# A two-layer hybrid decoder trunk: another way of finding the instruction order of four engines

## The chip, the cores and the metric

The kernel runs on one core of one Trainium2 chip, in one launch. The metric is the device time of that launch in microseconds (us). TensorE (PE) does the matrix products and transposes, VectorE (DVE), ScalarE (ACT) and GpSimd (POOL) the rest; transfers are issued by SyncE (SP), and a few by ScalarE. Every engine takes its instructions in the order of its own list, and waits at the head of the list until what the instruction needs is done.

## The reference

Two layers over one sequence of 1024 tokens of width 1024, all in f32. A layer normalises its input, projects it to 3088 columns, which three groups of heads share, and projects their outputs back:

```python
mod = c_act @ w_mod + b_mod                       # c_act = silu(c), one row
shift, scale, gate = jnp.split(mod[:, None, :], 3, axis=-1)
h = rms_norm(x, pre_gain) * (1.0 + scale) + shift
proj = h @ w_in                                   # split into aq..ag, rq..rg, gq..gg, ga
a_out = sliding_window_attention(rotary(aq), rotary(ak), av, sinks) * silu(ag)   # 8 heads, window 128
r_out = rms_norm(retention(rotary(rq), rotary(rk), rv)) * silu(rg)               # 4 heads, chunks of 128
log_a = log_sigmoid(ga @ gla_gate_w + gla_gate_b) / 16
g_out = rms_norm(gated_linear_attention(gq, gk, gv, log_a), gla_norm_gain) * silu(gg)   # 4 heads
y = concat([a_out, r_out, g_out]) @ w_out
x = x + gate * rms_norm(y, post_gain)
```

The modulation `mod` depends on `c` alone, but its weights w_mod are 1024 x 3072 for each layer.

## The kernel before

**Tiles.** The tokens lie in 8 tiles of 128. Every product of f32 values is done as products of a rounded high part and a low part in fp32r (`hi`, `lo`), three passes of TensorE in all. The high and low parts of weights and of the normalised, transposed input lie in two large arenas (`arena`); a weight is brought by a transfer into a stage buffer (`st`, 128 x 512 f32, 256 KB), and converted: `hi` by a copy (L149 on ScalarE, L151 or L529 on VectorE), `lo` by a subtraction (L533, on VectorE or GpSimd). All through the kernel there are five stage buffers (BST = 5) in rotation.

**Stages of a layer.** `pre` makes the normalised input of a tile: squares (L651), the sums (L640, L634), a power on GpSimd (L635), the scaling (L666), transposes on TensorE (L180), the modulation (L698, L700) and its split into high and low (L704, L708). Then come the projections of twelve column groups. Around them: SiLU gates (L984, L986), the decays of the gated-linear heads (`gla_decays`, L1038 to L1059), the rotation of queries and keys (`rotary`, L817 to L822; decay factor L1148) with tables that the kernel computes itself (L432 to L449), retention (L1170 to L1191), the gated-linear core (`gla_core`: 32-column products on TensorE, masked copies L1112, state L1133, L1134), attention by runs of tiles (L833 to L934), and the output projection, norm and residual (L1198 to L1239). Finished heads go through DRAM (`mixS`, `mixF`).

**Modulation.** The gate of layer 0 and the whole modulation of layer 1 are computed beside the projections, as sums on VectorE: each 256 KB piece of w_mod comes through a stage buffer, and one instruction (L362, L364) multiplies it by a column of `c_act` and adds it to `acc`:

```python
for k in range(KT):
    wt = stage()
    dma("lwm", wt, w_mod[l, j, hh, :, k, :])
    if k == 0 and j < 2:
        V.tensor_scalar(acc, wt, c_act[:, k:k + 1], None, ALU.mult)
    else:
        V.scalar_tensor_tensor(acc, wt, c_act[:, k:k + 1], acc, ALU.mult, ALU.add)
    yield lat("mod2", l)
```

**What sets the order.** The program is written as one stream of TensorE work and a set of jobs (generators). A clock that counts TensorE's cost decides when a job goes on (`pump`, with the delays of the table `L`; `mod2` is 4.0), and so where its instructions stand in the program. For TensorE, program order is the order on the chip (`manual_schedule` for PE). For the other engines and for the transfers the tile framework's scheduler chooses the order when the program is built: it takes instructions whose inputs it holds to be ready by a model of time, and inserts the waits. Buffers of a pool are handed out again when their last reader is done, so a transfer into a stage buffer waits for the instruction that read it last. The transfers lie on eight lanes, and on each lane one waits until the one ahead of it has landed.

## Time and profile before

| | |
|---|---|
| median of 3 runs | 1000.36 us (999.89 to 1002.28) |
| profiled execution | 1005.29 us, its span 1003.6 us |
| granted TensorE clock, mean | 0.989 |
| TensorE busy | 972.6 us, 97% of the span |
| VectorE busy | 683.7 us, 68% |
| ScalarE busy | 409.0 us, 41% |
| GpSimd busy | 234.7 us, 23% |
| VectorE waiting for pieces of w_mod at L364 | 12.0 us in 11 waits, longest 3.2 us |

The profile shows one execution. Its page gives the busy time of each engine, the chain of work that ended last, the groups of instructions by line and tile, and the transfers. A line number is that of the listing; helpers such as `copy` (L149, L151), `dma` (L154), `mult` (L165) and `transp` (L180) stand for many callers, which the tile's name tells apart. The timeline gives instructions in order of time with the idle time ahead of each and what ended it; the windows give busy time of the engines by stretch.

### The profile page before, as it was taken

How to read it: one execution, taken by the hardware profiler on the slowest of the kernel's cores; microseconds unless marked ns; L12 is line 12 of the kernel's file. 1: busy time of each engine (PE TensorE's matmuls, PEld its weight loads, DVE VectorE, ACT ScalarE, POOL GpSimd, SP SyncE). 2: the span in 40 equal slices, each digit the busy share in tenths (PEclk: the TensorE clock that was granted, in tenths of full speed). 3: DMA queues.
4: the chain of work that ended last, by engine and by line, in shares of the span. 5: the costliest groups of instructions: out<-in, count | busy, mean ns of one | idle time of the engine just before them, and what ended most of it. 6: DMA issues, size and time to landing. Idle time of an engine off the chain costs nothing.

```text
span 1003.6 us, 19610 instructions
## 1 busy us (share of the span) xinstructions
PE 972.6 (97%) x7137; PEld 827.5 (82%) x7137; DVE 683.7 (68%) x1680; ACT 409.0 (41%) x1152; POOL 234.7 (23%) x275
## 2 busy tenths in 40 slices
PE   5899999999999999999999999999999999999896
PEld 1599999888998777778889999998999777777675
DVE  3788857678666778654677385775766577566786
ACT  2486312233332656632555332133333267563231
POOL 2310001223320234420122010122332034444000
PEclk8899999999999999999999999999999999999998
DMA  8842513623235355597555241352222435477883
GB/s 306 297 145 79 166 43 102 189 78 121 65 94 172 90 156 168 167 283 234 178 171 166 82 139 32 117 171 68 64 82 88 122 91 153 129 227 237 252 272 132
DMA packets 112172, 148.73 MB, mean 148 GB/s; under 512 B 11998, under 2 KB 63688, under 8 KB 112076
## 3 DMA queue, kind: packets, MB, share of 16 engines
q1 hardware_dynamic: 106380, 137.92, 44.2%
q10 hardware_dynamic: 5696, 9.56, 2.6%
q8 instruction: 56, 0.92, 0.4%
q14 instruction: 40, 0.33, 0.1%
HBM read 109.17 MB, written 36.18 MB: 145 GB/s over the span
## 4 chain that ended last, share of the span: by engine, by line
PE 80%; DMA 8%; DVE 7%; issue 2%; POOL 1%; ACT 1%; SPq 1%; ACTq 0%; POOLq 0%; DVEq 0%
PE mm L165 62%; PE aux L165 14%; PE aux L180 5%; DMA st<-in_w_in_dram 2%; DMA st<-in_w_last_dram 1%; POOL sm L635 1%; DMA xk<-in_x_dram 1%; DMA a<-mixS 1%; DMA t<-aoS 1%; DMA t<-mixF 1%; DVE arena L533 1%; DVE t L328 0%; SPq L154 0%; DMA t<-in_x_dram 0%; DMA t<-xs 0%
## 5 line engine op out<-in xcount | busy, mean ns | idle before, releaser
L165 PE MATMUL mm<-arena 128*128 128x256 f32 (+2 forms) x1824 | 300.0, 318 | 1.8 <-ACT arena L704 1.8
L165 PE MATMUL mm<-arena,arena 128*128 128x256 f32 (+2 forms) x1824 | 299.0, 317 | 0.0
L165 PEld LDWEIGHTS mm<-arena 128*128 128x128 f32 x1824 | 255.3, 191 | 26.6 <-issue 4.1
L165 PEld LDWEIGHTS mm<-arena,arena 128*128 128x128 f32 x1824 | 252.9, 188 | 25.2 <-issue 4.4
L635 POOL TENSOR_TENSOR sm<-sm,mhalf 128x1 f32<-128x1 f32 (+1 forms) x64 | 55.8, 871 | 347.0 <-DVE sm L634 328.4
L165 PE MATMUL mm<-arena,mx 128*128 128x512 f32 (+1 forms) x564 | 132.6, 392 | 3.7 <-ACT kept L1332 3.7
L165 PEld LDWEIGHTS mm<-arena,mx 128*128 128x128 f32 x564 | 103.0, 190 | 28.2 <-ACT kept L1332 4.2
L149 ACT ACTIVATE t<-aux 128x256 f32<-128x256 f32 (+2 forms) x124 | 55.7, 467 | 74.9 <-PE aux L180 63.8
L149 ACT ACTIVATE arena<-st 128x512 fp32r<-128x512 f32 x94 | 55.9, 626 | 54.8 <-DMA st<-in_w_in_dram 19.7
L533 POOL TENSOR_TENSOR arena<-st,arena 128x512 fp32r<-128x512 f32 x31 | 43.3, 1399 | 134.1 <-ACT arena L149 96.8
L923 POOL TENSOR_TENSOR smx<-smx,sm 128x512 f32<-128x512 f32 x32 | 36.5, 1142 | 127.6 <-DVE sm L922 118.4
L533 DVE TENSOR_TENSOR arena<-st,arena 128x512 fp32r<-128x512 f32 x77 | 59.5, 794 | 4.5 <-ACT arena L149 2.4
L919 ACT ACTIVATE smx<-smx,sm 128x129 f32<-128x129 f32 x128 | 49.9, 392 | 28.8 <-DVE sm L916 28.8
L180 PE MATMUL aux<-c_ident,t 128*128 128x128 f32 (+1 forms) x292 | 48.8, 284 | 5.8 <-DVE t L666 5.5
L364 DVE SCALAR_TENSOR_TENSOR acc<-st,c_act,acc 128x512 f32<-128x512 f32 x60 | 45.5, 759 | 12.6 <-DMA st<-in_w_mod_dram 12.0
L180 PEld LDWEIGHTS aux<-c_ident,t 128*128 128x128 f32 (+1 forms) x292 | 35.4, 145 | 13.5 <-DVE t L666 7.4
L698 ACT ACTIVATE t<-aux,mod,mod 128x128 f32<-128x128 f32 x68 | 26.0, 460 | 44.5 <-DVE t L1239 18.3
L165 PEld LDWEIGHTS aux<-t,mx 32*128 32x128 f32 (+1 forms) x896 | 39.5, 187 | 3.9 <-issue 1.9
L967 ACT ACTIVATE t<-aux 128x256 f32<-128x256 f32 x32 | 12.3, 384 | 73.3 <-PE aux L165 60.7
L165 PE MATMUL aux<-t,mx 32*128 32x32 f32 (+1 forms) x896 | 40.6, 272 | 0.0
L914 DVE COPY_PREDICATED smx<-c_curmask,aux 128x256 f32<-128x256 int32 x64 | 25.5, 447 | 18.9 <-ACT smx L149 15.8
L1239 DVE SCALAR_TENSOR_TENSOR t<-t,sm,t 128x512 f32<-128x512 f32 x32 | 23.9, 779 | 17.9 <-DMA t<-in_x_dram 12.3
(220 smaller groups left out, 1378.2 us busy)
## 6 DMA issues: line engine op xcount, KB each, us to landing
st<-in_w_in_dram SPq DMA_DIRECT2D x96, 256.0 KB, 3.7
st<-in_w_mod_dram SPq DMA_DIRECT2D x64, 256.0 KB, 3.0
mx<-mixS SPq DMA_DIRECT2D x20, 512.0 KB, 5.8
mixS<-t SPq DMA_DIRECT2D x72, 128.0 KB, 2.6
st<-in_w_last_dram SPq DMA_DIRECT2D x36, 256.0 KB, 3.7
wm<-in_w_mod_dram SPq DMA_DIRECT2D x12, 512.0 KB, 7.2
t<-in_x_dram SPq DMA_DIRECT2D x24, 256.0 KB, 4.3
t<-tabS SPq DMA_DIRECT2D x16, 256.0 KB, 3.7
```

What stands on the lines that cost most here:

```text
L149: A.activation(dst, src, AF.Copy)
L165: T.matmul(dst, lhsT, rhs, start=start, stop=stop)
L180: T.transpose(dst, src, idn)
L364: V.scalar_tensor_tensor(acc, wt, c_act[:, k:k + 1], acc, ALU.mult, ALU.add)
L533: e.tensor_tensor(lo, st, f(hi), ALU.subtract)
L635: G.tensor_tensor(r, r, mhalf[:, :w], ALU.pow)
L698: A.activation(hf[:, ks], at[kt], AF.Identity, scale=gain, bias=shift)
L914: V.copy_predicated(sv, curmask.unsqueeze(1).to_broadcast((P, 2, P)), pv[:, :, n // P - 1, :])
L919: A.activation(sm[:, h, :], sm[:, h, :], AF.Exp, bias=mx[:, h:h + 1], accum_out=sums[:, h:h + 1])
L923: eng("pn").tensor_tensor(sm[:, :, 0:128], sm[:, :, 0:128], rs.unsqueeze(2).to_broadcast((P, 4, P)), ALU.mult)
L967: A.activation(sq, po, AF.Square)
L1239: V.scalar_tensor_tensor(xt[j], yg[j], r, xt[j], ALU.mult, ALU.add)
```

## The change

The context in which the whole program is built gets one option. With it, the scheduler that orders ScalarE, VectorE, GpSimd and the transfers finds out what is ready by playing the program through its timeline model, in place of the simple model of before. TensorE stays under `manual_schedule`. Tiles, buffers, arithmetic and the choice of the engine for each instruction are not touched.

```diff
-    with tile.TileContext(nc) as tc:
+    with tile.TileContext(nc, schedule_with_timeline_sim=True) as tc:
         with tc.manual_schedule(engines={mybir.EngineType.PE}):
             trunk(tc, ins, cst, out)
```

## The prediction

> **What bounds the kernel now.** I read the page first: the busy shares and the chain that ended last, then its groups of instructions and its transfer table.

> ```profile
> PE 972.6 (97%) x7137; PEld 827.5 (82%) x7137; DVE 683.7 (68%) x1680; ACT 409.0 (41%) x1152; POOL 234.7 (23%) x275
> PE 80%; DMA 8%; DVE 7%; issue 2%; POOL 1%; ACT 1%; SPq 1%; ACTq 0%; POOLq 0%; DVEq 0%
> L364 DVE SCALAR_TENSOR_TENSOR acc<-st,c_act,acc 128x512 f32<-128x512 f32 x60 | 45.5, 759 | 12.6 <-DMA st<-in_w_mod_dram 12.0
> st<-in_w_in_dram SPq DMA_DIRECT2D x96, 256.0 KB, 3.7
> st<-in_w_mod_dram SPq DMA_DIRECT2D x64, 256.0 KB, 3.0
> ```

> TensorE (PE) is busy 972.6 of the 1003.6 us, so all its waits together are 31 us: that is the most any order of the other engines could give back. TensorE's own order is written by hand and is the same in both builds. What the change can do, then, is to shorten these 31 us or to add to them. The third row names the danger. The modulation sums (L364) are on VectorE (DVE), each needs a 256 KB piece of w_mod that lands 3.0 us after its issue, and VectorE stands 12.0 us in front of them already. While it stands there everything behind it in its order stands too. Each piece is in one of five stage buffers, which the projection weights (w_in) use as well, and the next piece into a buffer is issued only when the last reader of that buffer is done. Where two pieces of w_mod follow each other through one buffer, their sums can't be closer than one round trip.

> Next I read the windows (stretch; length, busy us of PE, PEld, DVE, ACT, POOL; granted clock; DMA share; GB/s), to see where TensorE waits and what VectorE has in hand there.

> ```profile
> 0.00:25.00 25.00, 13.78 (x33) 4.77 (x34) 8.89 (x24) 6.23 (x13) 5.62 (x14) 0.88 0.87 306
> 25.00:50.00 25.00, 21.36 (x103) 13.78 (x102) 19.14 (x40) 11.63 (x31) 8.66 (x9) 0.85 0.84 296
> 75.00:100.00 25.00, 25.00 (x200) 24.01 (x200) 22.41 (x47) 16.59 (x38) 1.79 (x2) 1.00 0.25 77
> 300.00:525.00 225.00, 225.00 (x1227) 175.40 (x1226) 151.60 (x310) 110.04 (x330) 56.83 (x66) 1.00 0.58 181
> 950.00:1004.00 54.00, 45.27 (x205) 36.64 (x204) 39.31 (x74) 13.69 (x34) 4.37 (x6) 0.95 0.63 205
> ```

> Of the 31 us, 11.2 + 3.6 are in the first 50 us and 8.7 in the last 54. Between 300 and 525 us there is none, with VectorE two thirds busy: there, lateness of a few us costs nothing unless it passes the slack. From 75 to 100 us VectorE is busy 22.4 of 25 us, so what it loses before, it can't make up.

> **The change, part by part.** The instructions are the same, but for one table load of ScalarE (ACT) more. Put side by side, the two builds' lists differ on VectorE in 1599 of some 1620 lines, on SyncE (SP) in 503, on ScalarE in 471, on GpSimd (POOL) in 146, on TensorE in none. The one pattern I find is that instructions which consume a transfer, L364 and the weight conversions (L149, L151, L529, L533), come earlier, ahead of work that TensorE waits for. For each such place I take the durations of before, add what is newly ahead of the instruction TensorE needs, add the wait for a landing, and take off the slack it had.

> *Start-up.* The normalised tiles 2 and 3 (L666) feed TensorE's transposes.

> ```profile
> 44.86 0.88 DVE L666 TENSOR_SCALAR t<-mx,sm 128x512 f32<-128x512 f32 x2 [0.44 <-POOL sm L635]
> 46.99 1.88 DVE L666 TENSOR_SCALAR t<-mx,sm 128x512 f32<-128x512 f32 x2 [0.45 <-POOL sm L635]
> 48.53 1.09 PE L180 MATMUL aux<-c_ident,t 128*128 128x128 f32 x8 [0.65 <-DVE t L666]
> 37.69 10.60 SPq L715 DMA_DIRECT2D t<-in_x_dram  x8
> 49.76 0.76 SPq L772 DMA_DIRECT2D gnc<-in_gla_norm_gain_dram  x1
> ```

> TensorE already waits 0.65 us for the second pair, so there is no slack. Newly ahead of the first pair are 2.75 us of VectorE (two L529, an L151 and two L533 among them), of the second 2.19 us. Among these are L774, which needs gnc, and L151 of a weight piece. On SyncE gnc, three constants and that piece move past x loads, which in before were queued for 10.6 us. So 2.2 us is the work alone; if the loads come late too, 5. I take 3.0, nearer the work.

> *Tables and the first rotations.* L449 copies a table tile that TensorE transposes at 110.08.

> ```profile
> 106.35 0.27 DVE L820 TENSOR_TENSOR tr<-mm,sincos 128x128 f32<-128x128 f32 x1
> 107.95 0.41 DVE L449 COPY t<-sincos 128x512 f32<-128x512 f32 x1
> 110.08 0.60 PE L180 MATMUL aux<-c_ident,t 128*128 128x128 f32 x4
> 104.41 6.70 SPq L154 DMA_DIRECT2D st<-in_w_mod_dram  x4
> ```

> Three L364, one L533 and three rotary steps (3.32 us) are newly ahead of L449. The second L364 stands ahead of L820 too; its piece, issued at 104.41, lands at 107.4, 1.05 us after L820's old start. Slack was 110.08 − 108.36 = 1.72. That makes 3.32 + 1.05 − 1.72 = 2.65 us; if start-up backlog is still there, which the busy 75 to 100 us suggest, up to 8. I take 4.0.

> *The gated-linear heads at 220 us, the clearest place.* Masked copies (L1112) feed 32-column products at 223.17.

> ```profile
> 220.05 0.75 DVE L364 SCALAR_TENSOR_TENSOR acc<-st,c_act,acc 128x512 f32<-128x512 f32 x1 [0.27 <-DMA st<-in_w_mod_dram]
> 221.50 0.90 DVE L1112 COPY_PREDICATED mx<-c_mask,aux 128x128 f32<-128x128 int32 x4 [0.70 <-ACT mx L1111]
> 223.62 0.75 DVE L364 SCALAR_TENSOR_TENSOR acc<-st,c_act,acc 128x512 f32<-128x512 f32 x1 [1.23 <-DMA st<-in_w_mod_dram]
> 220.82 0.33 SPq L154 DMA_DIRECT2D st<-in_w_mod_dram  x1
> 224.40 4.83 SPq L154 DMA_DIRECT2D st<-in_w_mod_dram  x2
> 223.17 1.54 PE L165 MATMUL aux<-t,mx 32*128 32x32 f32 x48
> ```

> The rows show one buffer going round: sum at 220.05, next issue 220.82, next sum 223.62, next issue 224.40. That is 3.57 us a round. The other four buffers hold weights whose place in the arena TensorE hasn't left. In the new order three more L364 stand back to back ahead of the first L1112: at 223.6, 227.2 and 230.8. L1112 starts at 231.5 instead of 221.5, 10.0 us late. Its first copy had 1.4 us of slack, so TensorE stands still for 8.6 us. Nothing covers it, since TensorE's order is fixed. One more L364 stands ahead of the next group (L1077, L1078, L1087): of its 3.57 us I count 1.5.

> *What a standstill does to the clock.* The trace has a like one, at 940 us (the first row is the wait, the others are windows).

> ```profile
> 939.99 4.61 PE L165 MATMUL mm<-arena,mx 128*128 128x512 f32 x12 [3.72 <-ACT kept L1332]
> 940.00:941.00 1.00, 1.00 (x3) 0.86 (x4) 1.00 (x3) 0.00 (x0) 0.00 (x0) 0.71 0.54 149
> 941.00:942.00 1.00, 1.00 (x4) 0.71 (x4) 1.00 (x2) 0.39 (x1) 0.00 (x0) 0.50 0.79 192
> 942.00:943.00 1.00, 1.00 (x4) 0.81 (x3) 0.75 (x3) 0.33 (x2) 0.00 (x0) 0.50 0.72 195
> 943.00:944.00 1.00, 1.00 (x5) 0.77 (x4) 0.29 (x4) 0.00 (x0) 0.57 (x1) 0.58 0.88 276
> ```

> After 3.72 us without work the granted clock is 0.71, 0.50, 0.50 and 0.58: 0.29 + 0.50 + 0.50 + 0.42 = 1.7 us of work lost. I add 1.7 us once, for the standstill at 223. [...]

> *From layer 0 to layer 1.* On ScalarE three conversions L149, each waiting for its weight piece, are newly ahead of the squares (L651) of the next tiles; on VectorE an L364 and four L700 (2.03 us) are newly ahead of an L986.

> ```profile
> 529.01 0.62 ACT L651 ACTIVATE t<-t 128x512 f32<-128x512 f32 x1
> 525.39 9.37 SPq L154 DMA_DIRECT2D st<-in_w_in_dram  x7
> 538.56 0.41 DVE L986 SCALAR_TENSOR_TENSOR t<-t,mm 128x256 f32<-128x256 f32 x1
> 540.86 0.75 DVE L364 SCALAR_TENSOR_TENSOR acc<-st,c_act,acc 128x512 f32<-128x512 f32 x1 [0.61 <-DMA st<-in_w_mod_dram]
> 535.08 1.09 PE L180 MATMUL aux<-c_ident,t 128*128 128x128 f32 x8
> 540.26 1.05 PE L165 MATMUL mm<-arena 128*128 128x272 f32 x7
> ```

> L364 can't run before its landing at 540.86; with it (0.75) and the L700 (1.36) ahead, L986 starts at 543.0 and ends at 543.4, and TensorE wanted it at 540.26: 3.1 us. The third L149 waits for about 525.4 + 2 + 3.7 = 531, where L651 ran at 529.0; through L640, L634, GpSimd's power and L666 these 2 us reach the transposes at 535.08, which have no slack. Between 0 and 2.6 I count 1.4: together 4.5.

> *Rotations of layer 1.*

> ```profile
> 589.98 0.42 DVE L1148 TENSOR_TENSOR t<-t,c_kdec 128x256 f32<-128x256 f32 x1
> 593.28 0.60 PE L180 MATMUL aux<-c_ident,t 128*128 128x128 f32 x4
> 662.76 0.41 DVE L1148 TENSOR_TENSOR t<-t,c_kdec 128x256 f32<-128x256 f32 x1
> 665.75 0.60 PE L180 MATMUL aux<-c_ident,t 128*128 128x128 f32 x4
> ```

> Newly ahead of the first L1148 are four L364 and a rotary step, 3.15 us, with 2.9 us of slack: 0.3 us if all pieces have landed, 7.3 if each is issued as late as before. I take 2.0, since two of them free their buffers earlier too. Ahead of the second are 4.47 us (four L533, an L151, an L364 and two others) with 2.6 us of slack: 1.9.

> *At nothing* I cost the attention stretch, the mix stores and loads that SyncE reorders, GpSimd's changes and the added table load: the work that hides them is TensorE's unbroken 225 us and its like. If that cover is gone at one place it costs 1 to 3 us; the end part, where TensorE waits already, is the likeliest.

> The sum is 3.0 + 4.0 + 8.6 + 1.5 + 1.7 + 4.5 + 2.0 + 1.9 = 27.2 us on an execution of 1005.29, 2.7%. The runs shown have a median of 1000.36, so the profiled one is 0.5% above it; in the same proportion 1000.36 becomes 1027.

> **The rivals.**

> *Little of it counts (chance 0.18).* A standstill of TensorE lets VectorE catch up, and pieces issued earlier land earlier. Then the start (2.2 us) is left and, of 220 us, between a quarter of the 8.6 us and all of it with the 1.7 of clock: 4.4 to 12.5 us, 1005 to 1013. For it: the attention stretch swallows anything. Against it: the round of 3.57 us.

> *Everything counts (0.07).* Every upper end together: 5 + 8 + 8.6 + 3.6 + 1.7 + 5.7 + 7.3 + 1.9 is 42 us, and two or three waits more that pass the 3.7 us of the row at 940 add 1.7 each: 1042 to 1047. Against it: a late buffer is also one that TensorE has left.

> *Faster (0.13).* Transfers consumed earlier free their buffers earlier, so the next weights are there before TensorE asks. Its place is where TensorE waits in before: 0.65 us at 48.5, 3.72 + 1.7 at 940 and 8.7 in the last 54 us, 14.8 in all. If a fifth to a half of that goes and the round at 220 us doesn't form, because a second buffer is free there, it is 3 to 7 us faster, 993 to 997. It decides when L364 at 223.6 finds its piece landed. Against it: in before, with an order that freed buffers later, that instruction waited 1.23 us; and the first waits of the start-up hang on loads that don't move.

> *No difference (0.06).* TensorE at 97% hides all of it, or the moved instructions run in the same relative order where it matters: 997.4 to 1003.4. That the change does nothing is out, by the lists.

> **How the numbers follow.** The forecast, waits for landings ahead of work that TensorE needs, gets 0.56: 1027 by the sum; from 1014 (the low ends, half of the 8.6 us and no loss of clock: 2.2 + 2.65 + 4.3 + 3.1 + 0.3 + 1.9 = 14.4 us) to 1042 (the upper ends). 1000 to 1045 leaves out the faster case (0.13), part of no difference and most of the worst, together 0.2. A measurement of this kernel can tell about 0.3%, 3 us, from no change; faster by more 0.13, within 0.06, slower 0.81.

> **What would show it.** Right: TensorE's idle before L165 aux<-t,mx near 223 + shift at 7 us or more, ended by L1112, with VectorE waiting on three pieces of w_mod one after another and the clock at half after it; VectorE's wait for w_mod well above 12.0 us; TensorE's idle time near 58 us in all. Each place shows by its own row: L666 near 50, L449 near 115, L986 near 555, L1148 near 610 and 690. Wrong: TensorE's idle at or under 31 us, or L1112 released by ScalarE as before.

## The result, and the profile after

The changed kernel takes 1031.16 us (median of 4 runs, 1028.88 to 1034.67), the kernel before, in the runs set beside it, 1000.57 us: a ratio of 1.0303 (95% interval 1.0277 to 1.033). The forecast was 1027. The profiled execution of the changed kernel is its fastest, 1028.88 us with a span of 1027.1. The profiled execution of before that the prediction used (1005.29) is slower than its other runs, so I took a second profile of the same order (the kernel same_order, below; span 997.1). Times of single places are compared with that one.

The page of the changed kernel, in the same rows as before:

```profile
PE 979.5 (95%) x7137; PEld 832.8 (81%) x7137; DVE 692.3 (67%) x1680; ACT 408.6 (40%) x1153; POOL 236.1 (23%) x275
PE 72%; DVE 12%; DMA 9%; issue 3%; ACT 2%; POOL 1%; SPq 1%; DVEq 0%; POOLq 0%; ACTq 0%
L364 DVE SCALAR_TENSOR_TENSOR acc<-st,c_act,acc 128x512 f32<-128x512 f32 x60 | 47.4, 789 | 23.6 <-DMA st<-in_w_mod_dram 23.1
```

TensorE is idle 1027.1 − 979.5 = 47.6 us where it was 31 (25.7 in same_order). In the chain VectorE has gone from 7 to 12%, TensorE from 80 to 72. VectorE's wait for pieces of w_mod has gone from 12.0 us (13.6 in same_order) to 23.1 us. Both builds have the same instructions, but for the one table load more on ScalarE; what differs is their order.

TensorE's waits in its timeline name the places (start, duration, instruction, idle time ahead of it and what ended it):

```profile
49.41 2.22 PE L180 MATMUL aux<-c_ident,t 128*128 128x128 f32 x16 [1.50 <-DVE t L666]
101.31 0.66 PE L180 MATMUL aux<-c_ident,t 128*128 128x128 f32 x4 [0.98 <-DVE t L449]
115.60 0.66 PE L180 MATMUL aux<-c_ident,t 128*128 128x128 f32 x4 [1.41 <-DVE t L449]
236.03 2.95 PE L165 MATMUL aux<-t,mx 32*128 32x32 f32 x44 [8.01 <-DVE mx L1112]
265.66 0.67 PE L165 MATMUL aux<-stG,t 128*128 128x256 f32 x2 [1.47 <-DVE mx L1112]
323.33 0.30 PE L180 MATMUL aux<-c_ident,t 128*128 128x128 f32 x1 [1.20 <-DVE t L822]
556.40 1.09 PE L180 MATMUL aux<-c_ident,t 128*128 128x128 f32 x8 [1.50 <-DVE t L666]
612.08 3.95 PE L165 MATMUL mm<-arena 128*128 128x256 f32 x31 [0.51 <-DVE tr L820]
691.63 0.55 PE L180 MATMUL aux<-c_ident,t 128*128 128x128 f32 x3 [2.02 <-DVE t L1148]
858.73 0.65 PE L165 MATMUL aux<-t,vd 128*64 128x256 f32 x4 [0.85 <-POOL t L934]
```

Except the ones at 265, 323 and 858, each is a place of the prediction. At the clearest, VectorE's timeline shows the round of one stage buffer:

```profile
227.63 0.75 DVE L364 SCALAR_TENSOR_TENSOR acc<-st,c_act,acc 128x512 f32<-128x512 f32 x1 [1.13 <-DMA st<-in_w_mod_dram]
231.35 0.75 DVE L364 SCALAR_TENSOR_TENSOR acc<-st,c_act,acc 128x512 f32<-128x512 f32 x1 [2.97 <-DMA st<-in_w_mod_dram]
235.02 0.75 DVE L364 SCALAR_TENSOR_TENSOR acc<-st,c_act,acc 128x512 f32<-128x512 f32 x1 [2.91 <-DMA st<-in_w_mod_dram]
235.68 0.89 DVE L1112 COPY_PREDICATED mx<-c_mask,aux 128x128 f32<-128x128 int32 x4
```

Three sums stand 3.72 and 3.67 us apart, each waits about 3 us for its landing, and the masked copies that TensorE needs come behind them. The forecast was 3.57 us a round.

TensorE runs the same list in both, so the lateness of each of its instructions against same_order shows where the 29.8 us arose by which its last instruction is later (each row to about 0.3 us, by which instruction one takes at its edge):

| where (time in the order of before) | added, us | the prediction's term |
|---|---|---|
| start, to 50 us | 3.7 | 3.0 |
| tables and first rotations, to 115 us | 3.3 | 4.0 |
| 115 to 200 us | −0.6 | 0 |
| the standstill at 221 us | 8.5 | 8.6 |
| the stretch behind it, 222 to 226 us | 4.4 | 1.7 |
| 226 to 300 us | 1.2 | 1.5 |
| 300 to 530 us | 1.6 | 0 |
| layer 0 to 1, 533 us | 1.5 | 4.5 |
| rotations near 585 us | 1.2 | 2.0 |
| rotations near 665 us | 2.6 | 1.9 |
| 720 us to the end | 2.5 | 0 |

### The profile page after: what moved, and what is told of

It is laid out like the page before. It is cut to its first block, busy times and chain, and to the rows that moved or that the text cites. A ratio compares the mean times of both kernels' runs of the same rounds, so it can differ in the third digit from the quotient of the medians.

```text
span 1027.1 us, 19655 instructions
## 1 busy us (share of the span) xinstructions
PE 979.5 (95%) x7137; PEld 832.8 (81%) x7137; DVE 692.3 (67%) x1680; ACT 408.6 (40%) x1153; POOL 236.1 (23%) x275
## 4 chain that ended last, share of the span: by engine, by line
PE 72%; DVE 12%; DMA 9%; issue 3%; ACT 2%; POOL 1%; SPq 1%; DVEq 0%; POOLq 0%; ACTq 0%
PE mm L165 54%; PE aux L165 14%; PE aux L180 4%; DMA st<-in_w_mod_dram 2%; DMA wm<-in_w_mod_dram 2%; DVE arena L533 2%; DMA st<-in_w_last_dram 1%; DMA st<-in_w_in_dram 1%; DVE acc L364 1%; DMA t<-aoS 1%; DVE t L1239 1%; DMA t<-t 1%; DVE t L1077 1%; DMA t<-in_x_dram 0%; DMA a<-mixS 0%
## 5 line engine op out<-in xcount | busy, mean ns | idle before, releaser
L165 PE MATMUL mm<-arena 128*128 128x256 f32 (+2 forms) x1824 | 302.9, 320 | 2.7 <-ACT arena L704 1.8
L165 PE MATMUL mm<-arena,arena 128*128 128x256 f32 (+2 forms) x1824 | 300.4, 317 | 1.0 <-ACT t L149 0.7
L165 PEld LDWEIGHTS mm<-arena 128*128 128x128 f32 x1824 | 257.9, 193 | 27.9 <-issue 4.1
L165 PEld LDWEIGHTS mm<-arena,arena 128*128 128x128 f32 x1824 | 253.8, 189 | 26.6 <-issue 4.6
L165 PE MATMUL mm<-arena,mx 128*128 128x512 f32 (+1 forms) x564 | 131.0, 388 | 1.6 <-ACT kept L1332 1.4
L635 POOL TENSOR_TENSOR sm<-sm,mhalf 128x1 f32<-128x1 f32 (+1 forms) x64 | 54.4, 852 | 339.3 <-DVE sm L634 322.9
L165 PEld LDWEIGHTS mm<-arena,mx 128*128 128x128 f32 x564 | 101.7, 188 | 25.8 <-ACT kept L1332 1.8
L149 ACT ACTIVATE t<-aux 128x256 f32<-128x256 f32 (+2 forms) x124 | 55.4, 465 | 75.4 <-PE aux L180 63.0
L533 POOL TENSOR_TENSOR arena<-st,arena 128x512 fp32r<-128x512 f32 x31 | 45.9, 1485 | 158.4 <-ACT arena L149 109.7
L149 ACT ACTIVATE arena<-st 128x512 fp32r<-128x512 f32 x94 | 55.9, 627 | 43.9 <-PE mm L165 16.7
L533 DVE TENSOR_TENSOR arena<-st,arena 128x512 fp32r<-128x512 f32 x77 | 64.1, 866 | 2.8 <-PE mm L165 2.3
L180 PE MATMUL aux<-c_ident,t 128*128 128x128 f32 (+1 forms) x292 | 49.4, 284 | 17.0 <-DVE t L666 8.2
L364 DVE SCALAR_TENSOR_TENSOR acc<-st,c_act,acc 128x512 f32<-128x512 f32 x60 | 47.4, 789 | 23.6 <-DMA st<-in_w_mod_dram 23.1
L180 PEld LDWEIGHTS aux<-c_ident,t 128*128 128x128 f32 (+1 forms) x292 | 34.8, 144 | 26.5 <-DVE t L666 10.8
L165 PEld LDWEIGHTS aux<-t,mx 32*128 32x128 f32 (+1 forms) x896 | 42.2, 195 | 12.1 <-DVE mx L1112 8.1
L165 PE MATMUL aux<-t,mx 32*128 32x32 f32 (+1 forms) x896 | 43.4, 279 | 8.0 <-DVE mx L1112 8.0
## 6 DMA issues: line engine op xcount, KB each, us to landing
st<-in_w_in_dram SPq DMA_DIRECT2D x96, 256.0 KB
st<-in_w_mod_dram SPq DMA_DIRECT2D x64, 256.0 KB
st<-in_w_last_dram SPq DMA_DIRECT2D x36, 256.0 KB
t<-in_x_dram SPq DMA_DIRECT2D x24, 256.0 KB
t<-tabS SPq DMA_DIRECT2D x16, 256.0 KB
```

The lines of the kernel that those rows point to most:

```text
L149: A.activation(dst, src, AF.Copy)
L165: T.matmul(dst, lhsT, rhs, start=start, stop=stop)
L180: T.transpose(dst, src, idn)
L533: e.tensor_tensor(lo, st, f(hi), ALU.subtract)
L635: G.tensor_tensor(r, r, mhalf[:, :w], ALU.pow)
```

## The experiments

Most kernels below are the kernel before with its orders of VectorE, ScalarE, GpSimd and SyncE written down, as they stand in one of the two builds, and then edited. One helper does it; an edge of this kind sets the order of issue alone and adds no wait:

```python
def follow(tc, nc):                      # called behind trunk(...)
    at = {i.name: i for i in nc.cur_bb.bb.instructions}
    how = mybir.DependencyInfo(mybir.DependencyClass.NoSync, mybir.DependencyReason.DATA)
    for seq in ORDERS.values():          # one list of instruction names for each engine
        ns = [n for n in ("I-" + m for m in seq.split()) if n in at]
        for a, b in zip(ns, ns[1:]):
            tc.add_manual_dep(at[b], a, how, reason="order")
```

**The order of before, written down (same_order).**

```diff
+            follow(tc, nc)              # ORDERS: all four engines as in before
```

> The kernel before, with its own order of VectorE, ScalarE, GpSimd and the transfers written down as a chain of issue order. Both theories: no difference (ratio 0.998 to 1.002), since the order is the same; it shows what writing the order down costs by itself, and gives a second profile of the order of before. If TensorE's wait of 3.72 us at 940 us belongs to the order, it is there again; if it belongs to the one execution, the span is some 5 us shorter and the wait is not there.

Measured 1000.71 us, ratio 1.0006 (0.9992 to 1.0021): writing the order down costs nothing. The wait that stood at 939.99 us with 3.72 us in the first profile is here:

```profile
934.53 3.03 PE L165 MATMUL mm<-arena,mx 128*128 128x512 f32 x12 [0.28 <-ACT kept L1332]
```

The wait is 3.44 us shorter, and the 12 products behind it, then at half clock, took 4.61 us where they take 3.03: together 5.0 of the 6.5 us by which the two profiles of one order differ. They belong to that execution, and so does most of what lay between the profiled 1005.29 and the median.

**Three sums ahead of the masked copies, alone (three_ahead).**

```diff
 VectorE, order of before
+L364 st_3274, L364 st_3373, L364 st_3459
 L1112 x4 (aux_2708 to aux_2711)
-L364 st_3274 (behind L1112), L364 st_3373 (behind L1039), L364 st_3459 (behind L972)
```

> The order of before with one edit on VectorE: the three sums L364 of pieces st_3274, st_3373 and st_3459 stand ahead of the first masked copies L1112 near 221 us. Theory (a round of one stage buffer stands in front of L1112): TensorE waits 8 to 9 us before its 32-column products, then runs at half clock, which costs another 4.5 us as in the changed kernel: +12 to +14 us, ratio 1.012 to 1.014. Rival (VectorE catches up, or pieces come earlier when consumed earlier): at most +4 us, ratio under 1.004.

Measured 1011.77 us, ratio 1.0122 (1.0101 to 1.0143). TensorE and VectorE:

```profile
229.02 2.95 PE L165 MATMUL aux<-t,mx 32*128 32x32 f32 x44 [8.56 <-DVE mx L1112]
```

```profile
220.56 0.75 DVE L364 SCALAR_TENSOR_TENSOR acc<-st,c_act,acc 128x512 f32<-128x512 f32 x1 [2.78 <-DMA st<-in_w_mod_dram]
224.20 0.75 DVE L364 SCALAR_TENSOR_TENSOR acc<-st,c_act,acc 128x512 f32<-128x512 f32 x1 [2.89 <-DMA st<-in_w_mod_dram]
228.01 0.75 DVE L364 SCALAR_TENSOR_TENSOR acc<-st,c_act,acc 128x512 f32<-128x512 f32 x1 [3.05 <-DMA st<-in_w_mod_dram]
```

Three instructions of VectorE, moved ahead of four, make 1.2% of the kernel: 8.56 us of standstill, the rest behind it. The rival, that earlier consumption brings the pieces earlier, falls: rounds of 3.64 and 3.81 us, whatever waits behind them.

**A sixth stage buffer (three_ahead_6).**

```diff
-B2, B1, BS, BST, MMB, SMB = 10, 8, 11, 5, 3, 3
+B2, B1, BS, BST, MMB, SMB = 10, 7, 11, 6, 3, 3    # ORDERS as in three_ahead
```

> The order of the kernel three_ahead with six stage buffers in place of five (and seven small work buffers in place of eight, for the room). Theory (one circulating buffer sets the round): with two buffers going round only one landing is left to wait for, TensorE's standstill near 221 us shrinks from 8.5 to 2 or 3 us, the clock doesn't fall, and the ratio is 1.00 to 1.005. Rival (SyncE's order or the transfer itself sets the round): the standstill stays at 8 us and the ratio at 1.012 or more.

Measured 1008.27 us, ratio 1.0077 (1.0054 to 1.0099).

```profile
221.68 1.54 DVE L364 SCALAR_TENSOR_TENSOR acc<-st,c_act,acc 128x512 f32<-128x512 f32 x2 [2.82 <-DMA st<-in_w_mod_dram]
225.47 0.75 DVE L364 SCALAR_TENSOR_TENSOR acc<-st,c_act,acc 128x512 f32<-128x512 f32 x1 [2.26 <-DMA st<-in_w_mod_dram]
```

```profile
226.49 2.95 PE L165 MATMUL aux<-t,mx 32*128 32x32 f32 x44 [4.35 <-DVE mx L1112]
```

Two of the sums now run back to back (x2), one round is gone, and the standstill falls from 8.56 to 4.35 us. So the buffer sets the round, not SyncE. (That one small work buffer fewer costs nothing was not shown by itself.) The ratio lies between what the theory and what the rival had forecast: I had left only one landing to wait for; two are left, and the standstill of 4.35 us still brought the half clock (2.95 us for the 44 products), so the time fell less than expected.

**Filling the standstill (three_ahead_fill, three_ahead_fill36).** The extra products go behind the one 32-column product that doesn't wait:

```diff
                     mult(sp[h][:, P + 32 * s:P + 32 * s + 32], kxz[r, s - 1, c], ...)
+                    if (l, p, c, s, h) == (0, 0, 1, 1, 0):
+                        for _ in range(56):        # 36 in three_ahead_fill36
+                            T.matmul(sp[0][:, 256:384], ident, ident, start=True, stop=True)
```

> The order of the kernel three_ahead, with 56 extra 128x128 products of the identity on TensorE, written to an unused quarter of a PSUM tile, in the middle of the standstill. Theory (half clock after the standstill costs 4.5 us): TensorE stays at full clock, the 8.5 us of wait stay, and the time falls by 4 to 5 us against three_ahead, to a ratio of about 1.008 to 1.009. Rival (the slow stretch after the standstill has another cause, such as operands that come late): no gain, or a loss where the extra products reach past the standstill.

Measured 1014.26 us, ratio 1.0138 (1.0116 to 1.016), slower than three_ahead. I had mis-sized the products:

```profile
221.79 12.77 PE L1107 MATMUL aux<-c_ident 128*128 128x128 f32 x112
234.50 1.42 PE L165 MATMUL aux<-t,mx 32*128 32x32 f32 x43
```

They took 12.77 us and reached some 4 us past the first of the copies that TensorE waited for. Behind them the 32-column products ran in 1.42 us in place of 2.95. With the right number:

> As three_ahead_fill, with 36 extra products in place of 56: each took 0.228 us at full clock there (12.77 us for 56), so 36 take 8.2 us and end with the standstill. Theory: the clock stays full after the standstill and the time is 4 to 4.5 us under three_ahead, ratio 1.007 to 1.009. Rival (the slow stretch after the standstill isn't the clock): as three_ahead, 1.012.

Measured 1008.50 us, ratio 1.0075 (1.0055 to 1.0094), 3.3 us under three_ahead by the medians and 4.7 us by the ratios, each to the runs of before beside it: about the 4 to 4.5 expected, and the intervals don't touch.

```profile
220.66 8.30 PE L1107 MATMUL aux<-c_ident 128*128 128x128 f32 x72
229.11 1.80 PE L165 MATMUL aux<-t,mx 32*128 32x32 f32 x45
231.18 3.10 PE L165 MATMUL mm<-arena 128*128 128x256 f32 x24
```

The 24 products of 128x256 took 5.49 us in three_ahead and take 3.10 here, and the granted clock is 1.00 all through 219 to 240 us. The slow stretch behind the standstill was the clock.

**What brings the clock back (three_ahead_dense).**

```diff
+                    if (l, p, c, s, h) == (0, 0, 1, 1, 1):     # behind the product that waits
+                        for _ in range(26):
+                            T.matmul(sp[0][:, 256:384], ident, ident, start=True, stop=True)
```

> The order of three_ahead, with 26 extra 128x128 products of the identity on TensorE right behind the second 32-column product, that is right behind the standstill. In three_ahead the clock was down for 13.6 us, from 4.3 us after the last product before the standstill to 9.3 us after the first one behind it. Theory S (the small 32-column products hardly count as activity, dense ones do): the clock comes back one window of 3.4 us earlier, some 10.2 us after it fell, 6 us after the first product. Theory W (the clock comes back a fixed time after products start, whatever they are): 9.3 us after the first product, as in three_ahead. The extra products themselves cost 6 to 12 us, which is no verdict on the order.

One run, for its trace (1019.11 us, with the extra products). Windows of three_ahead, the first two, and of three_ahead_dense, the last two; the granted clock is the third number from the end:

```profile
224.00:226.00 2.00, 0.00 (x0) 0.00 (x0) 0.75 (x1) 0.00 (x0) 0.00 (x0) 0.68 0.02 4
238.00:240.00 2.00, 2.00 (x23) 1.84 (x22) 0.60 (x3) 0.77 (x2) 0.00 (x0) 0.91 0.00 0
```

```profile
226.00:228.00 2.00, 0.00 (x0) 0.00 (x0) 0.75 (x1) 0.00 (x0) 0.00 (x0) 0.88 0.00 0
237.00:238.00 1.00, 1.00 (x8) 1.00 (x8) 0.00 (x0) 0.00 (x0) 0.00 (x0) 0.62 0.00 0
```

All windows between are at 0.50. A mean of 0.68 over 2 us that begin at 1.00 and end at 0.50 puts the fall at 224.72; 0.91 puts the return at 238.36: 13.6 us. In the changed kernel the same reading gives 231.84 to 245.48, 13.6 us as well. With dense products (of 128 rows and columns) first it is 227.52 to 237.76: 10.2 us, 3.4 us less. A shorter spell of half clock in the changed kernel lasts 3.42 us (692.62 to 696.04, below); four times that are 13.7 us, three times 10.3, so these spells are whole multiples of it to 0.1 us.

How long the clock was down also went with how much of the standstill was left when it fell: 4.30 us in three_ahead, 4.19 in the changed kernel. In three_ahead_6, with the shorter standstill and 32-column products first, 0.65 us were left, and the same reading gives 225.84 to 236.08, 10.2 us:

```profile
225.00:226.00 1.00, 0.00 (x0) 0.00 (x0) 0.53 (x1) 0.00 (x0) 0.00 (x0) 0.92 0.04 14
236.00:237.00 1.00, 1.00 (x15) 0.84 (x15) 0.01 (x1) 0.00 (x0) 0.00 (x0) 0.96 0.00 0
```

So the time from TensorE's first product behind the standstill is what compares. It is 9.3 us in three_ahead (first product at 229.02), 9.4 in the changed kernel (236.03), 9.6 in three_ahead_6 (226.49) and 6.5 in three_ahead_dense (231.29): theory W falls. Counted from the first dense product (232.54, 239.55, 230.00 and 231.85) it is 5.8 to 6.1 us in all four. The 32-column products, though TensorE is listed as busy with them, did not bring the clock back: counted back from the return in steps of 3.41 us, the last step is in all four the first with dense products alone.

**The new order with the three sums put back (three_back).**

```diff
 VectorE, order of the changed kernel
-L364 st_3274, L364 st_3373, L364 st_3459
 L1112 x4 (aux_2708 to aux_2711)
+L364 st_3274 (behind L1112), L364 st_3373 (behind L1039), L364 st_3459 (behind L972)
-L364 st_3524 (behind L1112)
+L364 st_3524 (behind L1050)
 SyncE, order of the changed kernel
+t_483<-sgS, t_491<-sgS
 st_3524<-in_w_mod_dram
-t_483<-sgS, t_491<-sgS
```

> The changed kernel's order on all engines, with the four sums L364 of pieces st_3274, st_3373, st_3459 and st_3524 put back to where they stand in before (after the first L1112 group, after L1039, after L972, after L1050), and two loads of t from sgS ahead of the last of these pieces on SyncE. Theory: the standstill of 8 us, its half clock (4.5 us) and the 1 to 2 us near 265 us go, 13 to 14 us in all: ratio to before 1.016 to 1.018. Rival (the other moves of the new order take the place of this one, the next wait is as late): ratio 1.026 or more.

Measured 1024.87 us, ratio 1.0233 (1.0209 to 1.0258), between the theory and the rival: half of the gain that I expected. The place itself did as the theory said: no wait of TensorE over 0.3 us is left in its timeline between 187 and 253 us, and behind it, from 250 us on, its instructions come 11.9 us earlier than in the changed kernel. Up to the place the two profiles are 0.3 us apart (at 228 us): written down and built with the simple model, the order runs as in the build that found it. The 1.47 us near 265 stayed, though the fourth sum had been put back too, and further on other waits grew:

```profile
253.75 0.67 PE L165 MATMUL aux<-stG,t 128*128 128x256 f32 x2 [1.47 <-DVE mx L1112]
679.75 1.09 PE L165 MATMUL mm<-arena,arena 128*128 128x256 f32 x7 [3.04 <-DVE tr L820]
955.98 4.50 PE L165 MATMUL mm<-arena,mx 128*128 128x512 f32 x12 [2.15 <-ACT kept L1332]
```

The last one, with half clock (4.50 us for 12 products, 3.03 in same_order), is the wait that differs between executions of one order. Of the 11.9 us that the profile is ahead, 7.7 are left at TensorE's last instruction; 2.3 of the 4.2 us are lost at this row. From one profile I can't say how much of the gain that is missing is such chance and how much an answer of the order.

**One engine's order in the other build (dve_after, tl_dve_before).**

```diff
 dve_after
+            follow(tc, nc)              # simple model; ORDERS: VectorE alone, as in the changed kernel
 tl_dve_before
-    with tile.TileContext(nc) as tc:
+    with tile.TileContext(nc, schedule_with_timeline_sim=True) as tc:
+            follow(tc, nc)              # ORDERS: VectorE alone, as in before
```

> Built with the simple model as before; only VectorE's order is forced to that of the changed kernel, the orders of ScalarE, GpSimd and the transfers are found anew around it. Theory (VectorE's order carries the loss): +20 to +28 us, ratio 1.020 to 1.028, with the standstill near 221 us. Rival (the order of the transfers or of ScalarE carries it): under +10 us.

> Built with the timeline model as the changed kernel; only VectorE's order is forced to that of before, the other orders are found anew around it. Theory: 0 to +8 us, ratio 1.000 to 1.008, no standstill near 221 us; what is left is the start-up and ScalarE's part near 535 us. Rival (the transfers or ScalarE carry the loss): +15 us or more.

Measured 1056.92 us, ratio 1.0566 (1.0537 to 1.0595), and 1023.83 us, ratio 1.0234 (1.0189 to 1.028). Both theories missed, dve_after by twice what was forecast and tl_dve_before into the range of its rival (+15 us or more), and the pair does not say which engine's order carries the loss: a VectorE order under transfers ordered for another one seems to make losses of its own. In dve_after the start-up and the place of the masked copies show

```profile
55.86 3.91 PE L180 MATMUL aux<-c_ident,t 128*128 128x128 f32 x16 [7.52 <-DVE t L666]
245.32 2.95 PE L165 MATMUL aux<-t,mx 32*128 32x32 f32 x44 [7.88 <-DVE mx L1112]
```

The standstill at the masked copies goes with VectorE's order (7.88 us here, none in tl_dve_before). But tl_dve_before waits elsewhere, as long as that in sum. (Its profile is of the slowest of its four runs, which go from 1019.10 to 1032.37 us, so single waits of it may be chance.)

```profile
552.49 1.09 PE L180 MATMUL aux<-c_ident,t 128*128 128x128 f32 x8 [3.19 <-DVE t L666]
964.62 3.02 PE L165 MATMUL mm<-arena,mx 128*128 128x512 f32 x12 [2.45 <-ACT kept L1332]
979.19 4.46 PE L165 MATMUL mm<-arena,a 128*128 128x512 f32 x12 [3.18 <-DMA a<-mixS]
```

**Two other places alone (two_sites).**

```diff
 VectorE, order of before, two stretches sorted as in the changed kernel
+the 64 instructions of 94 to 121 us:     L533s, L151 and four L364 ahead of L1038, L1040, L817 to L822, L449
+the 39 instructions of 655.5 to 676 us:  L533 x4, L151, L364 ahead of L1148, L819 to L822
```

> The order of before with VectorE's list reordered as in the changed kernel at two places only: the 64 instructions that ran at 94 to 121 us, and the 39 at 655.5 to 676 us. Theory (each place costs by itself, through what is newly ahead of it): 2.6 to 3.5 us of new waits between 96 and 116 us, ended by L449 and L820, and 1.9 to 2.5 us between 660 and 680 us, ended by L1148 or L149; together 4.5 to 6 us, ratio 1.004 to 1.006. Rival (these places cost only together with the other moves, the start-up's backlog and SyncE's new order): at most 1.5 us, ratio 1.0015 or less.

Measured 1010.39 us, ratio 1.0103 (1.0083 to 1.0123), above what either had forecast.

```profile
106.34 1.09 PE L165 MATMUL mm<-arena 128*128 128x256 f32 x7 [0.73 <-DVE t L986]
114.10 0.66 PE L180 MATMUL aux<-c_ident,t 128*128 128x128 f32 x4 [1.73 <-DVE t L449]
674.14 1.84 PE L165 MATMUL mm<-arena,arena 128*128 128x256 f32 x7 [5.72 <-DVE tr L820]
```

The first place makes TensorE 3.2 us late, as expected. The second makes it 8 us late in place of 2, by a wait of 5.72 us and half clock behind it; 6.0 of them are left at 700 us. The timelines of VectorE and ScalarE show why:

```profile
670.04 0.69 DVE L533 TENSOR_TENSOR arena<-st,arena 128x512 fp32r<-128x512 f32 x1 [2.76 <-ACT arena L149]
669.37 1.32 ACT L149 ACTIVATE arena<-st 128x512 fp32r<-128x512 f32 x2 [2.82 <-DMA st<-in_w_in_dram]
```

L533 waits for a conversion, and that for a weight piece that SyncE still brings at its old place in its order. In the changed kernel SyncE and ScalarE had moved too, and the place cost 2.6 us. So these places do cost by themselves, and at the second one the new orders of the other engines make it cheaper, not dearer.

## Why the prediction was right

*The bound.* TensorE at 97% and in an order that can't give way: every late operand is paid in full. The sum of 27.2 us stands against 29.8 us in the trace. It comes out that close partly by luck, because terms that were too small and too large cancel. TensorE's idle time is 47.6 us, where I wrote 58. Two things make the difference: the 31 us that I started from held the wait at 939.99 us, and same_order has only 25.7; and of what was added, 8.1 us are not idle time but longer busy time (979.5 against 971.4), the slow stretch behind the standstill above all.

*The standstill at 221 us* (8.6 us forecast, 8.5 measured) is right in mechanism and size. Three sums moved by hand make it, a sixth buffer takes one round of it away, putting them back takes it away.

*The tables* (4.0, measured 3.3) are right; two_sites gives them alone 3.2 us. *The rotations of layer 1* (3.9, measured 3.8) are right in sum only: the first cost 1.2 us against 2.0, the second 2.6 against 1.9. Behind the second one's wait of 2.02 us (691.63) the granted clock was 0.50 for 3.4 us; I had counted half clock behind the standstill at 221 us alone.

*The fourth sum, 226 to 300 us* (1.5, measured 1.2), is right by luck. This L364 waits 2.14 us for its piece at 238.70, but TensorE has no wait over 0.3 us between the standstill and 265 us. The 1.47 us at 265.66 come at a later group of masked copies. In same_order that group stands right behind an L1078; here a third L533, two L1087, an L1039 and an L1042 are ahead of it too, and VectorE has no idle time before it:

```profile
263.50 0.89 DVE L1039 TENSOR_TENSOR_SCAN t<-c_rmask,t 128x256 f32<-128x256 f32 x1
265.23 0.88 DVE L1112 COPY_PREDICATED mx<-c_mask,aux 128x128 f32<-128x128 int32 x4
```

*The half clock* is the term that was mis-sized: 1.7 us forecast, 4.4 measured. I took the price from a standstill with dense products behind it; here 32-column products came first, and the clock stayed down 9.4 us after TensorE started again.

*From layer 0 to layer 1* (4.5, measured 1.5). The part through L651 and L666 was right: 1.4 forecast, 1.50 us in the row at 556.40. The part through L364 and L986 (3.1) failed, because I kept the landing of L364's piece where it was in before:

```profile
557.31 0.75 DVE L364 SCALAR_TENSOR_TENSOR acc<-st,c_act,acc 128x512 f32<-128x512 f32 x1 [0.57 <-DMA st<-in_w_mod_dram]
560.35 0.41 DVE L986 SCALAR_TENSOR_TENSOR t<-t,mm 128x256 f32<-128x256 f32 x1
561.59 1.05 PE L165 MATMUL mm<-arena 128*128 128x272 f32 x7
553.68 0.33 SPq L154 DMA_DIRECT2D st<-in_w_mod_dram  x1
```

TensorE is 21 us later here than in the first profile, so L364 ran at what was 536, not 541, and its piece was issued 5 to 6 us earlier by that measure. In both profiles SyncE issues it in the moment in which one of GpSimd's subtractions L533 ends (537.97 there, 553.67 here): the buffer is free earlier, since the conversion comes earlier. That is the mechanism of the rival "faster"; here it took away a loss, and nowhere did it bring TensorE a gain of more than 1.3 us.

*The start* (3.0, measured 3.7) is right only in sum. L666 made TensorE wait 1.50 us against 0.29 in same_order; most of the rest arose before 25 us, where I had costed nothing: there TensorE, ahead of its product at 14.68, waits 2.70 us for a load that ScalarE issues at 10.99 (at 6.83 in same_order). Profiles that have the start of before differ there by up to 2.9 us (three_ahead is 0.7 us earlier than same_order at 50 us, two_sites 2.2 later), so part of it may be chance.

*At nothing* I had costed what came to 4.1 us: 1.6 us in the attention stretch that I called unbroken (1.20 of it the wait for L822 at 323.33), and 2.5 us from 720 us on, which I had named as the likeliest place of such a loss.

*The count of lines.* The 1599 differing lines of VectorE are not 1599 moved instructions: in the written-down orders another instruction stands in 866 of 1680 places. Nothing in the sum rests on this count.

## What to carry to other kernels

Where an in-order engine consumes transfers through few buffers, don't put two consumers of one buffer next to each other ahead of work that the bounding engine waits for: each costs a whole round trip, here 3.6 to 3.8 us. When such an order is priced by hand from a trace, move the issue of a transfer with the instruction that frees its buffer, and let neither the landing nor the wait stay where it was. A standstill of the bounding engine is to be priced with the clock behind it, by what runs first after it (here half clock for 9.3 to 9.6 us with 32-column products first, for 6.5 with dense ones); and the order of one engine should be taken over with the orders of the others for which it was found: alone it cost more here, not less (dve_after, two_sites).

## What the runs showed of the hardware

Of the standstills shown here, those of 3.04 us and more brought half clock (behind the one of 3.04 us, in three_back, 14 products of 128x256 took 3.10 us, in same_order 1.92); of the shorter ones 2.02 us (the changed kernel) and 2.15 us (three_back, 12 products in 4.50 us) did and 2.45 us did not (tl_dve_before, 12 products in 3.02 us). So the length of one wait alone does not decide it in these runs. The changed kernel around the wait of 2.02 us:

```profile
689.20:692.60 3.40, 1.39 (x12) 1.15 (x11) 3.33 (x13) 0.39 (x1) 0.00 (x0) 1.00 0.77 232
692.00:693.00 1.00, 1.00 (x9) 1.00 (x8) 0.97 (x4) 0.77 (x2) 0.00 (x0) 0.81 0.90 312
696.00:697.00 1.00, 1.00 (x6) 0.91 (x7) 1.00 (x3) 0.38 (x1) 0.35 (x1) 0.98 0.93 238
```

The clock falls at 692.62 and is back at 696.04, 3.42 us later; in the 3.4 us ahead of the fall TensorE was busy for 1.39. This fall lies 460.8 us behind that of the long standstill (231.84), which is 135 steps of 3.413 us, and that one 191.2 us, 56 such steps, behind a fall at 40.68: these three falls lie on one grid. Why the wait of 2.45 us brought no half clock was not shown.

Two executions of one order can differ by 5.0 us at one place: a wait for ScalarE's L1332 of 3.72 us with half clock behind it, or of 0.28 us without.
